# A hybrid decoder step: conditioning weights in rows of 256 columns, norm parameters on another queue, two tiles' split weights in another pool

## The chip, the core and the metric

The kernel runs on one core of a Trainium2 chip. Its time is the device time of one execution in microseconds (us), smaller is better. The engines are named as the profile names them: PE is TensorE's matrix multiply and PEld its weight load, DVE is VectorE, ACT is ScalarE, POOL is GpSimd, SP is SyncE. A "q" behind a name (SPq) is the engine's sequencer or DMA queue. Each engine carries out its own instructions in order; engines wait for each other through semaphores. SP and GpSimd issue the DMA transfers of this kernel.

## What is computed

One step of a decoder layer with 1024 features (D) for 512 prompt tokens and 8 sample tokens, 520 columns in all. Cut to what matters here:

```python
cs = silu(c)                                  # 9 conditioning vectors: 1 prompt, 8 samples
mod = cs @ w_mod + b_mod                      # (9, 6*1024)
sh1, sc1, g1, sh2, sc2, g2 = split(mod, 6)
h = rmsnorm(x, norm1_g) * (1 + sc1) + sh1
u = h @ w_in                                  # 8 parts of 1024 columns
...                                           # HGRN2 and RG-LRU on the parts of u
x = x + g1 * (merged @ w_out)
h2 = rmsnorm(x, norm2_g) * (1 + sc2) + sh2
x = x + g2 * (square(relu(h2 @ w_ff1)) @ w_ff2)
y = rmsnorm(x, final_norm_g)
```

The first norm needs sc1 and sh1, parts 1 and 0 of `mod`: 2048 columns of `w_mod`, 8 MiB of float32.

## The kernel before, in words

Activations lie transposed: features over the 128 partitions in 8 column tiles (`KO` = 8), tokens along the free axis. A product with fp32 accuracy is made of three: weight and activation are each split into a high part (rounded to the fast fp32r type) and a low part (the rest), and TensorE adds high x high, high x low and low x high (`products`, L115). A weight tile of 1024 x 128 comes in by one transfer from SP (`_load_w`, L66, buffer `wst`, 4 of them), ScalarE casts the high part (L75) and VectorE subtracts for the low part (L78), which makes `whi` and `wlo`. `split_place` says where these go: pool `whl` has two places, 0 and 2, taken in turn; later, when pool `sw` is open, four places are taken in turn. A tile of weights is 48 TensorE instructions, in two halves of 260 columns.

The head of the program is `begin`. It loads c (L325, L326) and x (L391, L393), then the conditioning weights: `load_mod(k)` (L1432) fills one of 8 buffers `wm` (`NWM`) of 1024 x 256, with 128 columns of part 1 and 128 of part 0 for column tile k, by two transfers. In between stand the loads of the first two weight tiles of `w_in` (columns f and q of the first head). `parameters_mod` (L276) loads `b_mod`, `norm1_g` and `norm2_g` by three small transfers from SP into a tile `ra`; `bounds` (L232, L233) loads two other small tensors from GpSimd into a tile of the same name, which has one buffer in the pool, and `parameters` (L293 to L300) loads the rest, also from GpSimd. `parameters_mod_in` transposes the first of these (L222) into `pm`.

`mod` makes one group of conditioning products (L356): 16 matmuls for two column tiles. ScalarE evacuates them (L358), TensorE transposes (L372), VectorE reduces (L376) and adds bias and gain (L380) into `modT`. The first group is followed by `scale_x` (L415, L417), which multiplies x by its row scales; `transposed(k)` (L426, L427) turns a column tile of x round. Four groups (`LEAD`) are written ahead of `transposed_s` (L434), which turns the sample rows; the other four stand in the loop over column tiles. There `affine_split(k)` makes the operand tile h[k] (ACT L447; DVE L448, L449; the 8 sample columns on POOL L443 to L445), and `products` of the first two weight tiles follow for column tile k, into two accumulators `mm` in PSUM.

Then `begin` closes pool `start`, which holds x, `wm` and the small tiles, and opens `hg` over the same memory; the first writers of `hg` are two memsets on GpSimd (L1481, L1484), the load of the first head's state (L458) and the sigmoids of the first head (L137), which also empty the first accumulator, so that the third weight tile can use it. From there eight heads follow, each with the state update on VectorE and ScalarE beside TensorE's products, then branches, output projection and the MLP, whose weights come in under a plan of their own (`schedule`), which starts from the places that the last splits took.

The order of the instructions on each engine is made by the build, from priorities and a simulated timeline; `behind` and `issue_after` pin single ones.

Of the kernel before, what the change touches and what calls it, by code (L numbers as in the profile page):

```python
# [6 lines left out]
F32 = mybir.dt.float32  # L7
F32R = mybir.dt.float32r
# [3 lines left out]
OP = mybir.AluOpType  # L12
# [8 lines left out]
KO = D // 128  # L21
# [8 lines left out]
NWM = 8  # L30
# [18 lines left out]
class Kernel:  # L49
# [31 lines left out]
    def split_place(self):  # L81
# [1 line left out]
        self.nsplit += 1  # L83
        self.places.append(self.nsplit % 4 if self.sw else 2 * (self.nsplit % 2))
        return self.places[-1]

    def load_split(self, key, stage):
        return self._split_w(self._load_w(key, stage), self.split_place())

    def take_w(self, key):  # L90
        n = self.wcur
# [179 lines left out]

    def parameters_mod(self):

        r = self.start.tile([64, 128], F32, name="ra")
        for a, b, name in ((0, 48, "b_mod"), (48, 56, "norm1_g"), (56, 64, "norm2_g")):
            self.nc.sync.dma_start(r[a:b], self.rows8(self.i[name]))  # L276
        return r

    def parameters_mod_in(self, r):
# [1140 lines left out]
    def begin(self):  # L1420

        nc = self.nc
        self.start = self.open_pool("start", 1)
        self.load_c()
        self.identity()
        mk = [((1, k), (0, k)) for k in range(KO)]
        raw = {}

        def load_mod(k):
            raw[k] = self.start.tile([128, KO, 256], F32, name="wm", bufs=NWM)  # L1430
            for j, (w, r, c, _) in enumerate(self.mod_key(*p) for p in mk[k]):
                nc.sync.dma_start(raw[k][:, :, j * 128:(j + 1) * 128],  # L1432
                                  w[r:r + 1024, c:c + 128].rearrange("(k p) n -> p k n", p=128))

        self.load_x()
        self.cond()
        self.bounds()
        pm = self.parameters_mod()
        load_mod(0)
        first = [self.load_split(self.head_cols(0)[0], self.wst)]  # L1440
        load_mod(1)
        first.append(self.load_split(self.head_cols(0)[1], self.wst))
        for k in range(2, KO):
            load_mod(k)
        self.norm_x()
        self.constants()
        par = self.parameters()
        self.decays()
        self.parameters_mod_in(pm)
        evac = self.mod(mk[0], raw.pop(0))  # L1450
        with self.tc.issue_after(evac.ins):
            self.scale_x()
        x = [self.transposed(k) for k in range(3)]
        for k in range(1, LEAD):
            self.mod(mk[k], raw.pop(k))
        hi, lo = (self.act.tile([128, KO, T2], F32R, tag="h", name="h", bufs=2) for _ in range(2))
        self.h = [(hi[:, k, :T], lo[:, k, :T]) for k in range(KO)]
        pss = self.transposed_s()
        xs = self.start.tile([128, KO * NB], F32, name="xhs")
        nc.vector.tensor_copy(xs, pss[:, :KO * NB])  # L1460
        acc = [self.pmm.tile([128, 2, 512], F32, name="mm") for _ in range(2)]
        for k in range(KO):
            if k + LEAD < KO:
                evac = self.mod(mk[k + LEAD], raw.pop(k + LEAD))
            if k + 3 < KO:
                x.append(self.transposed(k + 3))
            self.split_last = self.affine_split(k, x[k], xs[:, k * NB:(k + 1) * NB])
            if k:
                for j in (0, 1) if k == 1 else (k,):
                    for ps, (wh, wl) in zip(acc, first):  # L1470
                        self.products(ps, (wh[:, j], wl[:, j]), self.h[j], j == 0, j == KO - 1)
                        self.behind(self.last_product, evac)
        self.parameters_in(*par)
        self.first = acc
        self.close_pool()
        self.hg = self.open_pool("hg", 2)
        self.ppt_free = False
        self.at = []
        self.fkq = [self.hg.tile([128, 3, 32], F32, name=f"fkq{n}", bufs=1) for n in range(2)]
        for t in self.fkq:  # L1480
            nc.gpsimd.memset(t, 0.0)  # L1481
        for n in range(2):
            a = self.hg.tile([128, NC, C], F32, name=f"at{n}", bufs=1)
            nc.gpsimd.memset(a, 0.0)  # L1484
            self.at.append(a)
# [54 lines left out]
```

## Time and profile before

| what | value |
|---|---|
| median of 3 runs | 1044.82 us (1044.5 to 1045.27) |
| the profiled execution, in all | 1044.54 us |
| its span, from first to last instruction | 1042.6 us |
| TensorE (PE) busy | 1005.1 us, 96% |
| VectorE / ScalarE / GpSimd busy | 694.9 / 526.1 / 112.8 us |
| bytes read from HBM | 123.61 MB |
| mean granted TensorE clock | 0.996 |

How to read what follows. In a timeline a line has start, duration, engine, line of the code, operation, output and inputs with their shapes, and the count of merged instructions; in brackets how long the engine sat idle before it and what ended that. In a group of instructions the columns are busy time, mean duration in ns, idle time before them and what ended most of it. The chain of waits is the work that ended last, followed back from the end. In a list of waits stand the total, the number and the longest. A DMA stretch gives packets, bytes and the mean rate; a queue's line gives packets, MB and the share of 16 engines' time (transfers overlap, so it can be over 100%).

### The profile page before, as it was taken

How to read it: one execution, taken by the hardware profiler on the slowest of the kernel's cores; microseconds unless marked ns; L12 is line 12 of the kernel's file. 1: busy time of each engine (PE TensorE's matmuls, PEld its weight loads, DVE VectorE, ACT ScalarE, POOL GpSimd, SP SyncE). 2: the span in 40 equal slices, each digit the busy share in tenths (PEclk: the TensorE clock that was granted, in tenths of full speed). 3: DMA queues.
4: the chain of work that ended last, by engine and by line, in shares of the span. 5: the costliest groups of instructions: out<-in, count | busy, mean ns of one | idle time of the engine just before them, and what ended most of it. 6: DMA issues, size and time to landing. Idle time of an engine off the chain costs nothing.

```text
span 1042.6 us, 24269 instructions
## 1 busy us (share of the span) xinstructions
PE 1005.1 (96%) x9940; PEld 968.5 (93%) x9940; DVE 694.9 (67%) x1583; ACT 526.1 (50%) x1020; POOL 112.8 (11%) x215
## 2 busy tenths in 40 slices
PE   2999999999999999999999999999999999999995
PEld 1799999999999999989999999999999999999994
DVE  7558688695867768465333337767767676777775
ACT  5445753573574456342122224366555655656653
POOL 2200000000000000020000000011422231232040
PEclk9999999999999999999999999999999999999998
DMA  9963344343434324496555578332572484274242
GB/s 277 260 178 107 110 134 115 112 136 114 126 116 126 113 82 135 137 312 178 163 157 157 157 217 234 93 97 67 124 181 70 100 174 125 52 158 96 62 81 83
DMA packets 247792, 143.71 MB, mean 138 GB/s; under 512 B 6622, under 2 KB 242326, under 8 KB 247674
## 3 DMA queue, kind: packets, MB, share of 16 engines
q1 hardware_dynamic: 237874, 130.28, 44.1%
q0 software_dynamic: 9808, 11.89, 6.3%
q8 instruction: 78, 1.28, 0.5%
q14 instruction: 32, 0.26, 0.1%
HBM read 123.61 MB, written 11.26 MB: 129 GB/s over the span
## 4 chain that ended last, share of the span: by engine, by line
PE 90%; DMA 3%; SPq 3%; ACT 1%; DVE 1%; issue 1%; DVEq 0%; ACTq 0%
PE mm L115 65%; PE ps L1085 8%; PE pt L1085 4%; PE pb L1085 2%; PE ps L356 2%; SPq L1432 2%; PE pb L702 1%; PE ps L561 1%; DMA wst<-in_w_branch_a_dram 1%; DMA wst<-in_w_in_dram 1%; DMA wm<-in_w_mod_dram 1%; PE mm L1085 1%; PE pt L645 1%; PE pt L634 1%; PE ps L529 1%
## 5 line engine op out<-in xcount | busy, mean ns | idle before, releaser
L115 PE MATMUL mm<-h,whi 128*128 128x260 f32 (+1 forms) x3072 | 513.9, 286 | 1.4 <-ACT X L137 1.4
L115 PEld LDWEIGHTS mm<-h,whi 128*128 128x128 f32 x3072 | 427.3, 188 | 7.0 <-issue 3.4
L115 PE MATMUL mm<-h,wlo 128*128 128x260 f32 (+1 forms) x1536 | 316.4, 285 | 0.0
L75 ACT CAST whi<-wst 128x1024 fp32r<-128x1024 f32 x168 | 175.8, 1048 | 228.9 <-PE mm L115 175.4
L78 DVE TENSOR_TENSOR wlo<-wst,whi 128x1024 fp32r<-128x1024 f32 x168 | 205.1, 1222 | 91.2 <-ACT whi L75 90.1
L115 PEld LDWEIGHTS mm<-h,wlo 128*128 128x128 f32 x1536 | 240.0, 189 | 1.5 <-issue 1.0
L115 PE MATMUL mm<-a,whi 128*128 128x260 f32 x512 | 84.6, 285 | 0.0
L115 PEld LDWEIGHTS mm<-a,whi 128*128 128x128 f32 x512 | 70.6, 188 | 1.4 <-issue 1.4
L115 PE MATMUL mm<-a,wlo 128*128 128x260 f32 x256 | 52.3, 284 | 0.0
L797 POOL DMA_DIRECT2D t<-oaT_d x8 | 4.3, 550 | 399.2 <-ACT ma L137 389.0
L1181 DVE TENSOR_TENSOR f<-f 128x260 f32<-128x260 f32 x64 | 27.3, 427 | 28.3 <-ACT f L1176 27.6
L1170 ACT ACTIVATE ft<-ft,fsh 128x512 f32<-128x512 f32 (+2 forms) x36 | 24.0, 676 | 36.0 <-DVE ft L1167 36.0
L115 PE MATMUL mm<-b,whi 128*128 128x260 f32 x256 | 41.8, 285 | 0.0
L1173 POOL TENSOR_TENSOR ft<-ft,fsh 128x8 f32<-128x8 f32 x28 | 17.6, 629 | 219.0 <-DVE ft L1167 219.0
L115 PEld LDWEIGHTS mm<-a,wlo 128*128 128x128 f32 x256 | 39.5, 188 | 0.2 <-issue 0.2
L115 PEld LDWEIGHTS mm<-b,whi 128*128 128x128 f32 x256 | 35.0, 188 | 1.6 <-issue 1.6
L1215 POOL DMA_DIRECT2D ma<-snap x28 | 27.2, 971 | 35.2 <-issue 30.9
L1197 POOL DMA_DIRECT2D ma<-snap x28 | 26.2, 935 | 43.6 <-DMA ma<-snap 28.1
L813 DVE TENSOR_TENSOR t<-mm,t 128x520 f32<-128x520 f32 x8 | 5.6, 700 | 36.7 <-PE ps L372 36.7
L1176 ACT ACTIVATE f<-ft 128x520 f32<-128x520 f32 (+1 forms) x36 | 20.8, 587 | 14.4 <-POOL ft L1174 12.3
L376 DVE TENSOR_REDUCE mods<-ps 128x9 f32<-128x36 f32 x32 | 6.1, 192 | 31.4 <-PE ps L372 31.3
L115 PE MATMUL mm<-b,wlo 128*128 128x260 f32 x128 | 25.9, 283 | 0.0
(488 smaller groups left out, 1876.4 us busy)
## 6 DMA issues: line engine op xcount, KB each, us to landing
wst<-in_w_in_dram SPq DMA_DIRECT2D x64, 512.0 KB
wst<-in_w_mod_dram SPq DMA_DIRECT2D x32, 512.0 KB
wst<-in_w_ff_dram SPq DMA_DIRECT2D x64, 256.0 KB
wst<-in_w_ff_dram SPq DMA_DIRECT2D x32, 512.0 KB
wm<-in_w_mod_dram SPq DMA_DIRECT2D x16, 512.0 KB
st<-in_state_hgrn_dram SPq DMA_DIRECT2D x8, 512.0 KB
vb<-vd SPq DMA_DIRECT2D x8, 512.0 KB
out_dram<-st SPq DMA_DIRECT2D x8, 512.0 KB
```

Source lines behind the costliest of these rows:

```text
L75: ins = self.nc.scalar.copy(hi, st)
L78: self.nc.vector.tensor_tensor(lo, st, hi.bitcast(F32), OP.subtract)
L115: self.last_product = self.nc.tensor.matmul(ps[:, s, :c.stop - c.start], x, y[:, c], start=first and n == 0, stop=last and n == 2)
L356: nc.tensor.matmul(ps[r:r + 32, :n], self.cT[:, k, :], w[:, k, :], start=k < 4, stop=k >= KO - 4)
L1085: ins = self.nc.tensor.matmul(ps, x[:, w], y[:, f], start=j in (1, 7, 2) and k == 0 and n == 0, stop=k == 3 and n == 2, skip_group_check=True)
L1170: nc.scalar.activation(t[:, :p], t[:, :p], AF.Relu, bias=sh[:, 0:1])
L1173: eng.tensor_tensor(t[:, p:], t[:, p:], sh[:, 1:9], OP.add)
L1176: nc.scalar.activation(f, self.two(self.ft)[:, a:a + n], AF.Square)
L1181: self.nc.vector.tensor_tensor(f[:, n], f[:, a], f[:, b], op)
L1197: nc.gpsimd.dma_start(x[1][:, b], v[:, :n], accum_op=OP.add)
L1215: nc.gpsimd.dma_start(x[t][:, a], s[p], accum_op=OP.add)
L1432: nc.sync.dma_start(raw[k][:, :, j * 128:(j + 1) * 128], w[r:r + 1024, c:c + 128].rearrange("(k p) n -> p k n", p=128))
```

## The change

`mk`, the list of pairs that make a conditioning group, is regrouped: a group holds two neighbouring column tiles of one part, part 1 and part 0 in turn, where it held one column tile of both parts. So a `wm` buffer is 256 neighbouring columns and is loaded by one transfer. `parameters_mod` is called first, issues on GpSimd's queue and has a tile name of its own. The first two weight tiles are split into tiles of pool `start` by `first_w`, and no longer take a place through `split_place`. Their loads stand behind the second and third conditioning load instead of the first and second.

```diff
-    def load_split(self, key, stage):
-        return self._split_w(self._load_w(key, stage), self.split_place())
-
...
-        r = self.start.tile([64, 128], F32, name="ra")
+        r = self.start.tile([64, 128], F32, name="rm")
         for a, b, name in ((0, 48, "b_mod"), (48, 56, "norm1_g"), (56, 64, "norm2_g")):
-            self.nc.sync.dma_start(r[a:b], self.rows8(self.i[name]))
+            self.nc.gpsimd.dma_start(r[a:b], self.rows8(self.i[name]))
...
-        mk = [((1, k), (0, k)) for k in range(KO)]
+
+        mk = [((part, k), (part, k + 1)) for k in range(0, KO, 2) for part in (1, 0)]
         raw = {}
 
-        def load_mod(k):
-            raw[k] = self.start.tile([128, KO, 256], F32, name="wm", bufs=NWM)
-            for j, (w, r, c, _) in enumerate(self.mod_key(*p) for p in mk[k]):
-                nc.sync.dma_start(raw[k][:, :, j * 128:(j + 1) * 128],
-                                  w[r:r + 1024, c:c + 128].rearrange("(k p) n -> p k n", p=128))
-
+        def load_mod(n):
+            raw[n] = self.start.tile([128, KO, 256], F32, name="wm", bufs=NWM)
+            w, r, c, _ = self.mod_key(*mk[n][0])
+            nc.sync.dma_start(raw[n], w[r:r + 1024, c:c + 256].rearrange("(k p) n -> p k n", p=128))
+
+        def first_w(j):
+            st = self._load_w(self.head_cols(0)[j], self.wst)
+            hi, lo = (self.start.tile([128, KO, 128], F32R, name=n, bufs=2) for n in ("whi", "wlo"))
+            nc.scalar.copy(hi, st)
+            nc.vector.tensor_tensor(lo, st, hi.bitcast(F32), OP.subtract)
+            return hi, lo
+
+        pm = self.parameters_mod()
         self.load_x()
         self.cond()
         self.bounds()
-        pm = self.parameters_mod()
         load_mod(0)
-        first = [self.load_split(self.head_cols(0)[0], self.wst)]
         load_mod(1)
-        first.append(self.load_split(self.head_cols(0)[1], self.wst))
-        for k in range(2, KO):
-            load_mod(k)
+        first = [first_w(0)]
+        load_mod(2)
+        first.append(first_w(1))
+        for n in range(3, KO):
+            load_mod(n)
```

## The prediction

> **What bounds the kernel now.** I read the page first, then the table of stretches, the chain of waits, and the timeline of the first 55 us.
>
> ```profile
> span 1042.6 us, 24269 instructions
> ...
> PE 1005.1 (96%) x9940; PEld 968.5 (93%) x9940; DVE 694.9 (67%) x1583; ACT 526.1 (50%) x1020; POOL 112.8 (11%) x215
> ```
>
> TensorE is busy for 96% of the span. The table of stretches (length; busy time and instructions of PE, PEld, DVE, ACT, POOL; clock; DMA share; GB/s) shows where the other 37 us lie.
>
> ```profile
> 0.00:17.00 17.00, 1.30 (x10) 1.18 (x10) 10.46 (x65) 8.98 (x16) 6.50 (x17) 1.00 0.93 270
> 17.00:53.00 36.00, 30.81 (x285) 22.03 (x285) 21.67 (x62) 17.50 (x29) 7.97 (x28) 1.00 1.08 264
> ...
> 55.00:300.00 245.00, 244.09 (x2827) 235.32 (x2826) 182.10 (x505) 132.30 (x293) 0.00 (x0) 1.00 0.43 123
> ...
> 680.00:1000.00 320.00, 319.69 (x2632) 319.47 (x2631) 229.15 (x364) 189.46 (x340) 80.72 (x135) 1.00 0.46 110
> ```
>
> The body idles 0.9 us in 245 and 0.3 in 320, so a microsecond saved ahead of it should reach the end, and none can be saved in it. The head is another matter: 15.7 us idle before 17 us, 5.2 more up to 53, with the DMA engines full. The chain of waits agrees: it runs through the issue queue of the conditioning weights (L1432) and one of their transfers.
>
> ```profile
> 27.38 1.74 SPq L1432
> 29.16 7.62 DMA wm<-in_w_mod_dram
> ...
> 38.57 2.88 PE mm L115 x24
> ...
> 54.27 15.62 PE mm L115 x128
> ```
>
> TensorE's timeline in the head, with idle time in brackets:
>
> ```profile
> 16.95 0.34 PE L222 MATMUL ps<-ident,ra 64*128 64x64 f32 x1 [9.91 <-DMA ra<-in_norm_g_dram]
> ...
> 25.85 1.07 PE L356 MATMUL ps<-wm,cT 128*32 128x256 f32 x16 [1.20 <-DMA wm<-in_w_mod_dram]
> ...
> 29.45 1.07 PE L356 MATMUL ps<-wm,cT 128*32 128x256 f32 x16 [0.32 <-DMA wm<-in_w_mod_dram]
> 30.45 0.66 PE L434 MATMUL ps<-ident,xsn 8*128 8x8 f32 x8
> ...
> 36.91 1.07 PE L356 MATMUL ps<-wm,cT 128*32 128x256 f32 x16 [1.07 <-DMA wm<-in_w_mod_dram]
> ...
> 44.23 1.07 PE L356 MATMUL ps<-wm,cT 128*32 128x256 f32 x16
> ...
> 52.47 0.41 PE L115 MATMUL mm<-h,wlo 128*128 128x260 f32 x2
> 54.27 0.75 PE L115 MATMUL mm<-h,whi 128*128 128x260 f32 x4 [1.40 <-ACT X L137]
> ```
>
> The third, fourth and sixth group of conditioning products start on a transfer's landing: 3.60 us apart for one pair of 524 kB tiles, 7.46 for two. At that pace the eighth lands at about 44.2, where its products start. Only after the fourth group can the sample rows be transposed (30.45), which the first complete operand tile needs; from there TensorE is nearly full to 52.88. So the head's end is the landing of the fourth pair plus TensorE's backlog behind it, with one wait on the sixth pair inside.
>
> **The change part by part.**
>
> *Rows of 256 columns.* The bytes stay at 8 x 1.049 MB; 16 transfers become 8, and a row grows from 512 to 1024 bytes. No transfer of the trace has rows of 1024 bytes. The nearest are the 512-byte stretch (12 to 40 us) and the one in which the prompt's rows of 4096 bytes load (4 to 9 us):
>
> ```profile
> DMA packets 16156, 8.15 MB, mean 291 GB/s; under 512 B 277, under 2 KB 16154, under 8 KB 16154
> ...
> q1 hardware_dynamic: 16152, 8.13, 120.2%
> ```
>
> ```profile
> DMA packets 775, 1.95 MB, mean 391 GB/s; under 512 B 191, under 2 KB 316, under 8 KB 775
> ...
> q1 hardware_dynamic: 597, 1.92, 97.4%
> ```
>
> One of 16 engines takes 16 x 28 us / 16152 = 27.7 ns for a packet of 503 bytes, and 16 x 5 us / 597 = 134 ns for one of 3216. A line through both is 8 ns a packet and 0.039 ns a byte; 1024 bytes then take 48 ns, or 340 GB/s. The bounds are 291 (the row length does nothing) and 391. I take 340, since the fixed part is what is halved. A pair then takes 3.08 us for 3.60: 0.52 us saved each (0 to 0.92). The fourth pair lands 4 x 0.52 = 2.1 us sooner (0 to 3.7), with as many bytes ahead of it as before, both weight tiles included. The sixth lands 3.1 sooner, 1.0 more than the backlog has moved, which leaves almost nothing of its 1.07 us wait: 1.0 more (0 to 1.1).
>
> [...]
>
> *Regrouping.* A pair of products now holds the scales of two column tiles, the next one their shifts. Same instructions; operand tile 4 now needs the sixth group where it needed the fifth. That costs nothing as long as the products of tiles 0 to 3 cover it: 48 at 2.88 us per 24, so 5.8 us, against the 3.7 us between the fifth group at about 33.2 (36.91 less one pair) and the sixth. Without the cover it would cost the 3.7.
>
> *Norm parameters on GpSimd's queue.* The 9.91 us wait at 16.95 is on three small transfers that stand on SP's queue behind a weight tile:
>
> ```profile
> 9.82 2.36 SPq L276 DMA_DIRECT2D ra<-in_b_mod_dram  x1
> ```
> ```profile
> 1.38 0.77 POOL L232 DMA_DIRECT2D ra<-in_hg_lower_dram  x1 [0.32 <-issue]
> ```
> ```profile
> DMA to landing us min/median/max: 3.1/3.8/4.5
> ```
> ```profile
> 8.00 0.19 ACT L245 ACTIVATE ptmp<-ptmp 128x8 f32<-128x8 f32 x1
> ```
>
> The second line is from the answer for the tile that these loads write: issue to landing. Ahead of GpSimd's other loads they land by about 1.4 + 3 x 0.77 + 4.5 = 8.2 us at the latest, and the first group waits only for its own pair, at 27.3 less three pairs and two weight tiles of 1.8 us: 14.5. TensorE can then do the prompt's transposes earlier, of which 16 still come after the fourth group:
>
> ```profile
> L426 PE MATMUL pb<-ident,xn 128*128 128x128 f32 x16 | 2.6, 283 | 0.5 <-ACT xn L427 0.5
> ```
>
> Whatever leaves the backlog is saved, 0 to 2.6 us; TensorE runs in the order that the build gave it, and scaling x still stands behind the first group, so I take 0.5. The three issues push the rest of GpSimd's queue back by three times at most 0.77 = 2.3 us: the two loads of L232/L233 first, behind which ScalarE's exponentials of 8.00 us stand ahead of two squares. The row scales then come up to 2.3 us later, still by about 17 us; cost 0, as a transfer at 29 decides. The parameters behind them are read after 45 us. SP loses three issues, but its queue is paced by full DMA engines, so nothing is gained there.
>
> *Split weights in the start pool.* Casts and subtractions of the first two tiles are the same ones, to another address; the first tile now loads behind the second pair, 3.1 us later, long before the products of 31 us. Tiles three and four no longer wait for the first two's buffers. The timelines of ScalarE, VectorE, GpSimd and SP at the seam:
>
> ```profile
> 52.17 1.05 ACT L75 CAST whi<-wst 128x1024 fp32r<-128x1024 f32 x1 [1.59 <-PE mm L115]
> 53.13 0.60 ACT L137 ACTIVATE e<-mm 128x520 f32<-128x520 f32 x1
> 53.62 0.60 ACT L137 ACTIVATE X<-mm 128x520 f32<-128x520 f32 x1
> ```
> ```profile
> 53.25 1.23 DVE L78 TENSOR_TENSOR wlo<-wst,whi 128x1024 fp32r<-128x1024 f32 x1 [1.57 <-ACT whi L75]
> ```
> ```profile
> 51.54 0.30 POOL L1481 MEMSET fkq<- 128x96 f32 x2 [0.90 <-DVE h L449]
> ```
> ```profile
> 51.50 0.37 SPq L458 DMA_DIRECT2D st<-in_state_hgrn_dram  x1
> ```
>
> The cast leaves the 1.40 us gap. But the next pool's first writers (memset, state load) start right after the last reader of the start pool; that reader is now the last product (52.88), no longer VectorE's last subtraction. The sigmoid that frees the accumulator writes a tile of that pool too, so it starts behind 52.88, and its pair takes 53.62 + 0.60 - 53.13 = 1.1 us plus a hop: I take 0.1 us gained (0 to 0.8, if it need not wait). The state load goes out 1.4 us later; behind it on SP stand the gate matrices and the seventh weight tile. Tiles three to six are loaded by then and give 4 x 48 products, 23 us of cover; if it were gone, the 1.4 us would show. The two early casts and subtractions (1.05 and 1.23 each) go into idle time, below with its releasers for 40 to 52 us:
>
> ```profile
> L447 ACT ACTIVATE h<-xn,modT 128x512 fp32r<-128x512 f32 x3 | 2.5, 818 | 6.5 <-DVE modT L380 6.5
> ```
> ```profile
> L376 DVE TENSOR_REDUCE mods<-pt 128x18 f32<-128x72 f32 x3 | 0.7, 233 | 5.3 <-PE pt L372 5.3
> ```
>
> Cost 0 there, up to 1.5 if they stand in front of the norm's own work. Later splits count from two less: the order of buffers shifts only where the third and fourth pair of buffers open, in a stretch without idle time; 0.
>
> *Sum.* 2.1 + 1.0 + 0.5 + 0.1 = 3.7 us less. The profiled execution took 1044.54 in all (1.94 outside its span), so 1040.8 for it; the median of the runs lies 0.28 above that execution, hence **1041.1**. By the bounds: 3.7 + 1.1 + 2.6 + 0.8 = 8.2 less, or 1.5 more: 1036.6 to 1046.3.
>
> **The rivals.**
>
> *The row length does nothing.* 291 GB/s stays, the fourth pair lands at 29.4, and 0.5 + 0.1 remain: 1044.2. For it: the DMA engines are full at 291 with packets all of one size, and the faster stretch also reads from another tensor. Against it: 27.7 and 134 ns leave room for a fixed part only.
>
> *Casts ahead of the norm.* ScalarE works in order, and in the trace it has already stood behind a cast whose tile had not landed:
>
> ```profile
> 16.02 1.04 ACT L75 CAST whi<-wst 128x1024 fp32r<-128x1024 f32 x1 [3.41 <-DMA wst<-in_w_in_dram]
> ```
>
> If both new casts stand ahead of the last evacuation, it waits for two tiles behind the eighth pair: 3.6 us of transfer and 1.05 of cast, then an estimated 2.9 for evacuation, transposes, reduction, affine step and split (two of them in the rows above; idle time between them not counted), and 2.88 for the last two tiles' products: 10.4 after a landing at 44.2 - 4.2 = 40.0. The end at 50.4 instead of 52.88 leaves 2.5 gained: 1042.3. Against it: the code traces the norm first.
>
> *A worse order in the heads (slower).* The build orders instructions by a simulated timeline, and the change moves its first 50 us. The list of waits shows one place where TensorE, in order, stands before a transpose (L534) for VectorE's last product of a head:
>
> ```profile
> PE pt L534 <- DVE e L663: 1.8, 3, 1.0
> ```
>
> It occurs in each of eight heads and costs in three. At the longest 1.0 in all eight it is 6.2 us more, and 2.5 more net: 1047.3. It outweighs the gain from four further heads on. For it: it is order alone that spares the other five. Against it: within the heads nothing is changed.
>
> **How the numbers follow.** Forecast 0.55 (with its own range 1038.8 to 1042.8: rates of 310 to 391), no gain from rows 0.22, casts ahead 0.10, worse order 0.13. A measurement of this kernel can tell about 0.2%, 2.1 us. Faster by more: 0.54 of the forecast and 0.06 of the casts, 0.60. Within: 0.22, 0.04 and some 0.02 of the rest, 0.28. Slower by more: 0.12. The range, 1037.0 to 1046.4, takes in the bounds and the first two rivals, and leaves out most of the last.
>
> **What would show it.** Eight transfers of 1 MB on L1432, with a rate near 340 GB/s where 291 stood; the parameters' transpose before 10 us and the first group near 14.5; the fourth group near 27.3; the last product of the first two tiles near 49.3; a gap of about 1.3 us behind it, with the sigmoids right after the last product. It is wrong if the rate stays at 291, if a cast stands on ScalarE behind a transfer between the last two evacuations, or if the stretch from the third tile to the end is over 1 us longer than now.

## The result, and the profile after

| | median, us | lowest to highest | executions |
|---|---|---|---|
| before | 1044.61 | 1043.88 to 1046.73 | 14 |
| changed | 1045.07 | 1042.11 to 1047.51 | 14 |

The ratio of changed to before is 1.0003, with an interval of 0.9993 to 1.0014: no difference that can be told. The predicted range holds the time; the predicted gain of 3.7 us isn't there. The changed kernel's executions spread over 5.4 us, those of before over 2.9. Its profiled execution took 1044.72 us in all, against 1044.54. Lines of the code up to `begin` count three less than before: L356 is now L353, L426 L423, L115 L112, L447 L444.

The page of the changed kernel, span and busy time:

```profile
span 1042.9 us, 24260 instructions
...
PE 1006.9 (97%) x9940; PEld 970.3 (93%) x9940; DVE 693.8 (67%) x1583; ACT 527.0 (51%) x1022; POOL 114.2 (11%) x218
```

The table of stretches, columns as before the change:

```profile
17.00:53.00 36.00, 31.75 (x283) 23.43 (x283) 24.46 (x93) 21.46 (x34) 7.06 (x24) 0.95 0.97 281
...
55.00:300.00 245.00, 244.32 (x2828) 235.61 (x2828) 180.62 (x504) 131.34 (x291) 0.00 (x0) 1.00 0.41 121
```

The body is as full as it was. In the head TensorE is busy for 0.9 us more and its granted clock is 0.95 where it was 1.00. The DMA engines between 12 and 40 us:

```profile
DMA packets 11003, 9.37 MB, mean 335 GB/s; under 512 B 219, under 2 KB 10945, under 8 KB 10993
```

That is 335 GB/s for 291, with weight tiles of 512-byte rows in the same stretch; where only the 1024-byte rows move, 26 to 28 us, it is 348. So the transfers did what was forecast. TensorE's timeline:

```profile
14.35 0.47 PE L423 MATMUL pb<-ident,xn 128*128 128x128 f32 x1 [10.28 <-DVE xn L414]
...
14.97 0.36 PE L219 MATMUL ps<-ident,rm 64*128 64x64 f32 x1
17.40 3.64 PE L353 MATMUL ps<-wm,cT 128*32 128x256 f32 x32 [2.07 <-DVE pl L220]
...
26.95 1.07 PE L353 MATMUL ps<-wm,cT 128*32 128x256 f32 x16 [0.87 <-DMA wm<-in_w_mod_dram]
...
39.81 1.07 PE L353 MATMUL ps<-wm,cT 128*32 128x256 f32 x16
...
47.01 0.43 PE L219 MATMUL ps<-ident,rd 96*128 96x96 f32 x2 [0.24 <-DVE pa L220]
...
48.99 0.51 PE L112 MATMUL mm<-h,whi 128*128 128x260 f32 x2 [0.72 <-DVE h L446]
...
50.43 1.50 PE L112 MATMUL mm<-h,whi 128*128 128x260 f32 x6
...
54.37 0.75 PE L112 MATMUL mm<-h,whi 128*128 128x260 f32 x4 [1.19 <-ACT X L134]
```

The fourth group starts at 26.95 (29.45 before) and the eighth at 39.81 (44.23), yet the third weight tile's first product starts at 54.37, where it started at 54.27. The gain was there at 27 us and had gone by 54. Where it went is read by laying the table of stretches from the end of the fourth group to the third tile side by side, first before, then changed:

```profile
30.45:54.27 23.82, 20.89 (x200) 17.06 (x196) 14.13 (x36) 10.08 (x19) 7.97 (x28) 1.00 1.00 247
```
```profile
27.95:54.37 26.42, 23.79 (x213) 19.95 (x209) 15.87 (x41) 13.84 (x24) 8.19 (x28) 0.94 0.86 244
```

The stretch is 2.60 us longer. TensorE is not idle in it for longer (2.63 for 2.93); it is busy for 2.90 more. Two things account for that. The groups of instructions in this stretch show 24 transposes of x behind the fourth group where 16 stood:

```profile
L423 PE MATMUL pb<-ident,xn 128*128 128x128 f32 x24 | 3.8, 275 | 0.0
```

The group's busy time was 2.6 us before, so eight more are 1.2 us. Two transposes of `mod` and two products of the first tiles have moved behind the fourth group with them. Neighbouring instructions overlap (24 at a mean of 275 ns are 6.6 us, against 3.8 of busy time), so the busy times of groups don't simply add up, and the 1.2 us stand as an estimate for all of these. Stretches of 2 us show the granted clock:

```profile
46.00:48.00 2.00, 1.67 (x13) 1.24 (x11) 1.86 (x8) 1.33 (x2) 0.88 (x4) 1.00 0.78 207
48.00:50.00 2.00, 1.28 (x9) 1.08 (x8) 1.55 (x4) 0.58 (x2) 0.00 (x0) 0.89 0.61 180
50.00:52.00 2.00, 2.00 (x11) 2.00 (x11) 0.00 (x0) 0.90 (x1) 0.00 (x0) 0.50 0.01 4
52.00:54.00 2.00, 1.18 (x6) 0.93 (x5) 0.14 (x1) 0.78 (x2) 0.76 (x4) 0.75 0.00 0
```

0.89 and 0.75 as means of 1 and 0.5 put the half clock at 49.56 to 53.0, 3.4 us, in which TensorE was busy throughout: half of that, 1.7 us, is lost, an estimate from the clock. The six products at 50.43 take 1.50 us; six such products took 0.97 before. (The column prints 1.00 also ahead of the first change of clock that was recorded. There the lengths of equal products tell more: in the kernel before, the first conditioning group at 17.21 takes 1.93 us and the third at 25.85 takes 1.07. By the lengths of the groups between, an estimate, TensorE came to its full clock at about 20.9 us before and at 22.3 in the change.) 1.2 + 1.7 = 2.9, the further busy time. So 2.5 us from the landing and 0.3 of idle time were gained, 2.9 were lost, and the head of the traced execution ends 0.1 us later.

ScalarE, GpSimd and SP of the changed kernel at the seam:

```profile
41.04 1.05 ACT L75 CAST whi<-wst 128x1024 fp32r<-128x1024 f32 x1 [0.54 <-DMA wst<-in_w_in_dram]
42.00 0.36 ACT L355 COPY modev<-ps 128x256 f32<-128x256 f32 x1
...
46.66 1.52 ACT L444 ACTIVATE h<-xn,modT 128x512 fp32r<-128x512 f32 x2 [2.31 <-DVE modT L377]
49.61 1.28 ACT L134 ACT_TABLE_LOAD   x1 [1.42 <-DMA wst<-in_w_in_dram]
53.22 0.60 ACT L134 ACTIVATE e<-mm 128x520 f32<-128x520 f32 x1 [2.32 <-PE mm L112]
```
```profile
53.24 0.30 POOL L1486 MEMSET fkq<- 128x96 f32 x2 [5.66 <-PE mm L112]
```
```profile
53.21 0.37 SPq L455 DMA_DIRECT2D st<-in_state_hgrn_dram  x1
```

The first sigmoid, the next pool's memset and the state's load all start right behind the last product (53.18), as forecast. A cast stands ahead of the last group's evacuation (42.00), and one step, L444 at 46.66, makes two operand tiles out of that group. The table load at 49.61 wasn't forecast. Its cause stands on ScalarE earlier:

```profile
18.40 1.04 ACT L1435 CAST whi<-wst 128x1024 fp32r<-128x1024 f32 x1 [5.80 <-DMA wst<-in_w_in_dram]
19.46 1.28 ACT L242 ACT_TABLE_LOAD   x1
20.76 0.21 ACT L242 ACTIVATE ptmp<-ptmp 128x8 f32<-128x8 f32 x1
```

The exponentials, at 8.00 before, now stand behind the table load on the line of a sigmoid (L402, 1.28 us at 11.10). A further load of 1.28 us stands right ahead of them, at 19.46, and one more ahead of the first head's sigmoids, at 49.61. The kernel before has the load of L402 (there L405, at 11.12) and neither of these two; with the exponentials back at 8.2 us, in an experiment below, both are gone.

### The profile page after: what moved, and what is told of

Its sections match the earlier page's. It is cut to its first block, busy times and chain, and to the rows that moved or that the text cites. A ratio compares the mean times of both kernels' runs of the same rounds, so it can differ in the third digit from the quotient of the medians.

```text
span 1042.9 us, 24260 instructions
## 1 busy us (share of the span) xinstructions
PE 1006.9 (97%) x9940; PEld 970.3 (93%) x9940; DVE 693.8 (67%) x1583; ACT 527.0 (51%) x1022; POOL 114.2 (11%) x218
## 3 DMA queue, kind: packets, MB, share of 16 engines
q8 instruction: 78, 1.28, 0.5%
## 4 chain that ended last, share of the span: by engine, by line
PE 90%; DMA 3%; DVE 3%; SPq 2%; ACT 1%; issue 1%; DVEq 0%; ACTq 0%
PE mm L112 65%; PE ps L1082 8%; PE pt L1082 4%; PE ps L353 2%; PE pb L1082 2%; PE pb L699 1%; DMA wm<-in_w_mod_dram 1%; PE ps L558 1%; DMA wst<-in_w_in_dram 1%; SPq L1430 1%; PE mm L1082 1%; PE pt L642 1%; PE pt L631 1%; SPq L66 1%; DVE wlo L78 1%
## 5 line engine op out<-in xcount | busy, mean ns | idle before, releaser
L112 PE MATMUL mm<-h,whi 128*128 128x260 f32 (+1 forms) x3072 | 515.5, 286 | 2.0 <-ACT X L134 1.2
L112 PEld LDWEIGHTS mm<-h,whi 128*128 128x128 f32 x3072 | 428.5, 189 | 7.2 <-issue 3.4
L112 PE MATMUL mm<-h,wlo 128*128 128x260 f32 (+1 forms) x1536 | 317.2, 285 | 0.0
L75 ACT CAST whi<-wst 128x1024 fp32r<-128x1024 f32 x166 | 173.7, 1048 | 220.4 <-PE mm L112 175.8
L78 DVE TENSOR_TENSOR wlo<-wst,whi 128x1024 fp32r<-128x1024 f32 x166 | 202.6, 1221 | 91.7 <-ACT whi L75 90.0
L112 PEld LDWEIGHTS mm<-h,wlo 128*128 128x128 f32 x1536 | 240.7, 189 | 2.0 <-issue 1.4
L112 PE MATMUL mm<-a,whi 128*128 128x260 f32 x512 | 85.1, 286 | 0.0
L112 PEld LDWEIGHTS mm<-a,whi 128*128 128x128 f32 x512 | 70.7, 188 | 1.4 <-issue 1.4
L112 PE MATMUL mm<-a,wlo 128*128 128x260 f32 x256 | 52.0, 284 | 0.0
L1178 DVE TENSOR_TENSOR f<-f 128x260 f32<-128x260 f32 x64 | 27.3, 426 | 28.9 <-ACT f L1173 28.2
L112 PE MATMUL mm<-b,whi 128*128 128x260 f32 x256 | 41.8, 285 | 0.0
L112 PEld LDWEIGHTS mm<-a,wlo 128*128 128x128 f32 x256 | 39.4, 188 | 0.2 <-issue 0.2
L112 PEld LDWEIGHTS mm<-b,whi 128*128 128x128 f32 x256 | 35.0, 188 | 1.6 <-issue 1.6
L519 ACT ACTIVATE st<-st,fkq 128x128 f32<-128x128 f32 x64 | 20.0, 390 | 13.0 <-DVE fkq L498 10.5
```

Source lines behind the costliest of these rows:

```text
L75: ins = self.nc.scalar.copy(hi, st)
L78: self.nc.vector.tensor_tensor(lo, st, hi.bitcast(F32), OP.subtract)
L112: self.last_product = self.nc.tensor.matmul(ps[:, s, :c.stop - c.start], x, y[:, c], start=first and n == 0, stop=last and n == 2)
L519: nc.scalar.activation(st[:, b], st[:, b], AF.Copy, scale=fkq[:, 0, b:b + 1])
L1178: self.nc.vector.tensor_tensor(f[:, n], f[:, a], f[:, b], op)
```

## The experiments

The first theory: the rows and the placing are worth what was forecast up to 27 us, and the head loses it again between 28 and 54 us, because the last two column tiles share one group and TensorE runs thin there. The rival: one of the other edits (parameters, pool) costs what the rows gain. Each edit was first run alone on top of the kernel before (median 1044.79 on that chip), beside the whole change with its last groups undone.

**The rows alone.**

```diff
-        mk = [((1, k), (0, k)) for k in range(KO)]
+        mk = [((part, k), (part, k + 1)) for k in range(0, KO, 2) for part in (1, 0)]
...
+            nc.sync.dma_start(raw[n], w[r:r + 1024, c:c + 256].rearrange("(k p) n -> p k n", p=128))
```

> The rows and the regrouping alone; norm parameters on SP and split weights in their old pool. If the rows carry the gain and the last group, which two column tiles now need, gives it back (first theory): a rate near 348 GB/s while the pairs load, the eighth group near 40 us instead of 44.2, TensorE idle by about 1 us between the last group's transposes and the last tiles' products, and in some executions a stretch of half clock of 3.4 us there: times spread over 1042 to 1047 as with the whole change. If the other two parts lose what the rows gain (rival): 1040.5 to 1042, with a spread as small as before's.

Measured: median 1044.48, ratio 1.0001 (0.9991 to 1.0012). TensorE's timeline:

```profile
27.40 1.07 PE L356 MATMUL ps<-wm,cT 128*32 128x256 f32 x16
...
49.51 0.50 PE L115 MATMUL mm<-h,whi 128*128 128x260 f32 x2 [0.70 <-DVE h L449]
...
50.57 0.88 PE L115 MATMUL mm<-h,whi 128*128 128x260 f32 x6
...
53.58 0.75 PE L115 MATMUL mm<-h,whi 128*128 128x260 f32 x4 [1.42 <-ACT X L137]
```

The fourth group is 2.05 us earlier, the third tile only 0.69. The wait of 0.70 ahead of the last products is there without the other edits, and so are the 24 transposes behind the fourth group, but not the half clock: six products take 0.88. From the end of the fourth group (28.40) to the third tile TensorE is busy for 22.68 us, 1.8 more than before, all of it at full clock. So the regrouping by itself gives back two thirds of the gain in this execution; of the 0.69 the execution kept nothing (span 1043.2), since from the third tile to the end it took 989.6 where before took 988.3.

**The parameters alone on GpSimd's queue**, first there.

```diff
-            self.nc.sync.dma_start(r[a:b], self.rows8(self.i[name]))
+            self.nc.gpsimd.dma_start(r[a:b], self.rows8(self.i[name]))
...
+        pm = self.parameters_mod()
         self.load_x()
         self.cond()
         self.bounds()
-        pm = self.parameters_mod()
```

> The norm parameters on GpSimd's queue alone. First theory: the front of the head has slack, the fourth group still lands at 29.4 us, 1044.2 to 1045.0, spread as before. Rival: the parameters' transpose moves behind those of x in TensorE's order and costs 1 us or more: above 1045.5.

Measured: median 1047.96 of five executions, ratio 1.0031 (1.0019 to 1.0043), slower by 3.2 us. The rival had the loss but another cause: the parameters' transpose runs at 9.40 us, ahead of the first of x at 14.49. ScalarE, then TensorE:

```profile
17.41 1.28 ACT L245 ACT_TABLE_LOAD   x1
...
54.78 1.28 ACT L137 ACT_TABLE_LOAD   x1
```
```profile
20.09 1.94 PE L356 MATMUL ps<-wm,cT 128*32 128x256 f32 x16 [2.27 <-DVE ptmp L247]
...
57.22 0.75 PE L115 MATMUL mm<-h,whi 128*128 128x260 f32 x4 [2.83 <-ACT X L137]
```

Here the second table load falls between the last product and the sigmoid, and the gap is 2.83 us in place of 1.40. The third tile is 2.95 later; the other half of that arose in the head, where the first load stands ahead of the exponentials, the second group waits 2.27 for VectorE's steps behind them and takes 1.94 us for 1.27, by its length at half clock. In the whole change the second load fell at 49.61, where ScalarE was idle, and cost nothing that the trace shows: its cover is that the casts have left this place.

**The pool alone.**

```diff
+        def first_w(j):
+            st = self._load_w(self.head_cols(0)[j], self.wst)
+            hi, lo = (self.start.tile([128, KO, 128], F32R, name=n, bufs=2) for n in ("whi", "wlo"))
...
-        first = [self.load_split(self.head_cols(0)[0], self.wst)]
+        first = [first_w(0)]
```

> The split weights in the start pool alone. First theory: the gap ahead of the third tile goes from 1.40 to about 1.2 us and nothing else moves: 1044.2 to 1044.8. Rival: the early casts stand on ScalarE in front of the norm's work and the memset, state load and sigmoids wait for the last product: 1045.5 or more.

Measured: median 1046.19, ratio 1.0012 (1.0003 to 1.002), slower by 1.4 us. ScalarE, then TensorE:

```profile
45.46 1.05 ACT L75 CAST whi<-wst 128x1024 fp32r<-128x1024 f32 x1 [2.20 <-DMA wst<-in_w_in_dram]
46.41 0.36 ACT L358 COPY modev<-ps 128x256 f32<-128x256 f32 x1
```
```profile
55.57 0.74 PE L115 MATMUL mm<-h,whi 128*128 128x260 f32 x4 [1.19 <-ACT X L137]
```

This is the rival of the casts ahead of the norm, with one of the two casts ahead of the evacuation: ScalarE waits 2.20 us for a weight tile's landing with the last group's evacuation behind it. The gap at the seam shrinks by 0.2, the third tile starts 1.3 later.

**The whole change, with the last two groups in the old form**, so that each of the last two column tiles has a group of its own:

```diff
-        mk = [((part, k), (part, k + 1)) for k in range(0, KO, 2) for part in (1, 0)]
+        mk = [((part, k), (part, k + 1)) for k in range(0, KO - 2, 2) for part in (1, 0)]
+        mk += [((1, k), (0, k)) for k in (KO - 2, KO - 1)]
```

> The whole change, but groups seven and eight in the old form (one column tile each, rows of 512 bytes). First theory: those two pairs land about 1 us later, but tile 6 no longer waits for the eighth group; TensorE's idle time of about 1 us in front of the last products goes, and with it the stretch of half clock: 1041.5 to 1043.5, spread under 2 us. Rival (the pairing of the last tiles is not the cause): 1044 to 1047 with the spread of the whole change.

Measured: median 1043.76, ratio 0.9989 (0.998 to 0.9998).

```profile
40.42 1.07 PE L353 MATMUL ps<-wm,cT 128*32 128x256 f32 x16 [0.64 <-DMA wm<-in_w_mod_dram]
...
52.48 0.75 PE L112 MATMUL mm<-h,whi 128*128 128x260 f32 x4 [1.24 <-ACT X L134]
```

The eighth group is 0.6 later than in the change and the third tile 1.9 earlier: no wait stands ahead of the last products, and the granted clock is 1.00 all through this stretch. Most of the 1.9 is the clock. From the end of the fourth group (27.85) to the third tile it takes 24.63 us, 0.8 more than before, where the change takes 2.6 more. So the waits go with the shared last group, and in the change the half clock came with it; the rows alone have the group without the half clock. The median agrees, though it lies a little above the 1041.5 to 1043.5 that were expected, and its interval overlaps that of the change. With the runs of the single edits, the rival holds as well: both of its costs are real where the edits stand alone. The next four kernels, on another chip (before: median 1045.42), took those costs away one by one.

**The whole change, parameters behind the bounds' loads on GpSimd:**

```diff
-        pm = self.parameters_mod()
         self.load_x()
         self.cond()
         self.bounds()
+        pm = self.parameters_mod()
```

> The whole change, but the three norm parameters stand on GpSimd's queue behind the two loads of bounds instead of ahead of them. Theory: ahead of them they push bounds' exponentials behind the change of ScalarE's table to the sigmoid, so that two more table loads of 1.28 us stand on ScalarE and bounds' work on VectorE and TensorE stands in front of the first group; behind them the exponentials run before 9 us again and both loads go. The parameters alone cost 3.2 us against before, so 1042 to 1044 here, the third tile 1 to 2 us sooner than in an execution of the whole change at full clock. Rival (the slack of the front hides this in the whole change): 1045, the same as the whole change.

Measured: median 1047.11, ratio 1.0014 (1.0005 to 1.0023): a miss. The table loads are gone, the exponentials are back at 8.2 us, and the first group starts 2.2 us sooner. But:

```profile
15.18 1.93 PE L353 MATMUL ps<-wm,cT 128*32 128x256 f32 x16
...
22.79 1.93 PE L353 MATMUL ps<-wm,cT 128*32 128x256 f32 x16 [2.06 <-DMA wm<-in_w_mod_dram]
...
27.63 1.94 PE L353 MATMUL ps<-wm,cT 128*32 128x256 f32 x16
...
54.62 0.74 PE L112 MATMUL mm<-h,whi 128*128 128x260 f32 x4 [1.19 <-ACT X L134]
```

All four early groups take 1.93 us in place of 1.07, the half clock's length, up to 29.5 us. With the wait of 2.07 us gone, TensorE's early work stands spread out, with idle time between the groups, where the change has two groups back to back. The third tile is no earlier than in the change. The execution that was traced was the fastest of the eleven, 1044.60 us; why the median lies 2.5 above it, no trace shows.

**The whole change, split weights in their old places** (the loads behind the second and third conditioning load, as in the change):

```diff
-        first = [first_w(0)]
+        first = [self.load_split(self.head_cols(0)[0], self.wst)]
```

> The whole change without the pool of its own: the first two tiles' split weights take places 2 and 0 again. Theory: the early casts of tiles three and four leave the norm's stretch, which took 1.3 us of the pool's own experiment, but the third tile's cast (1.05 us) and the table load (1.28 us) now stand between the last product and the sigmoid: gap 2.5 to 2.9 us instead of 1.2, in sum 1044.5 to 1046.5. Rival (the early casts cost nothing here): 1046 to 1047.

Measured: median 1045.72, ratio 1.0006 (0.9997 to 1.0015). ScalarE, then TensorE:

```profile
50.02 1.05 ACT L75 CAST whi<-wst 128x1024 fp32r<-128x1024 f32 x1 [2.39 <-PE mm L115]
51.09 1.28 ACT L137 ACT_TABLE_LOAD   x1
```
```profile
46.98 0.88 PE L115 MATMUL mm<-h,whi 128*128 128x260 f32 x4 [0.29 <-ACT h L447]
...
53.53 1.23 PE L115 MATMUL mm<-h,whi 128*128 128x260 f32 x4 [2.84 <-ACT X L137]
```

Cast and table load stand together in the gap, 2.84 us, after which TensorE runs at half clock (four products in 1.23 us for 0.75, and a granted clock of 0.50 from 54 to 58 us). So the own pool takes the cast out of the gap in the whole change, and gives the table load its cover. It has a price there too: without it the last products wait for 0.29 us, where the change waits for 0.24 and 0.72, and they end at 50.70 at full clock, 2.5 us before those of the change. This kernel has the shared last group as well, so how long the last products wait hangs on the order around it too. In the medians, 1.0006 and 1.0003 of the kernel before, the pool is neither a gain nor a loss that can be told.

**All three**: rows for six groups and the old form for the last two, parameters behind the bounds' loads, old places.

> Rows of 256 columns for six groups, the last two groups in the old form, norm parameters on GpSimd behind bounds' loads, old places for the first two tiles. Theory (each of the three losses has its own cause): no second table load, no early casts, no idle time ahead of the last products: third tile near 51.5, 1041 to 1042.5. Rival (the losses overlap or a new order brings its own): 1043 or more.

Measured: median 1043.4, ratio 0.9983 (0.9972 to 0.9994), 1.8 us faster than before by the ratio, the lowest of all kernels here, but above the 1041 to 1042.5 that were expected.

```profile
27.01 1.94 PE L356 MATMUL ps<-wm,cT 128*32 128x256 f32 x16
...
52.40 0.75 PE L115 MATMUL mm<-h,whi 128*128 128x260 f32 x4 [1.42 <-ACT X L137]
```

The third tile is 1.87 us earlier than before (near 51.5 was expected), and about as much arrives in the median, although the fourth group still takes 1.94 us, by its length at half clock.

**The same with the own pool.**

> As the last one, but with the pool of its own for the first two tiles' split weights. Theory: casts of tiles three and four stand on ScalarE in the norm's stretch again and cost up to 1.3 us there, against 0.2 us won at the gap: 0.5 to 1.2 us slower than with the old places, 1041.8 to 1043.5. Rival: the pool is worth its 0.2 us and is equal or faster.

Measured: median 1045.74, ratio 0.9998 (0.9986 to 1.001), 2.3 us above its sister on the same chip, though the two intervals overlap; 0.5 to 1.2 were expected. In the traced execution a wait for the norm's operand is back in the last products, and the third tile starts at 53.56, 1.16 later:

```profile
50.35 1.30 PE L112 MATMUL mm<-h,whi 128*128 128x260 f32 x6 [0.53 <-ACT h L444]
```

With no table load to cover, the pool looks like a loss, though not one clear of noise.

**An earlier full clock.** From the miss came a third theory: what the head lacks is TensorE at full clock from the first group on, and some work for it beforehand would give that, which the author assumed and no run had shown. Four kernels got 11 further products of the identity with the conditioning vectors, 256 columns each, at about 7 to 14 us, into an accumulator that nobody reads (before: median 1044.82 on that chip).

```diff
+        warm = self.cT.rearrange("p k b -> p (k b)")
+        pw = self.ppt.tile([128, 512], F32, name="pt")
+        for _ in range(11):
+            nc.tensor.matmul(pw[:, :256], self.ident, warm, start=True, stop=True)
         load_mod(0)
```

The change with it, the best version with it, the kernel before with it, and the change with parameters behind the bounds' loads with it:

> The whole change plus 11 products of the identity with the transposed conditioning (no result is used), on TensorE between the transposes of c and the first transposes of x, where it idles for 10 us. [...] With the extra products the full clock comes before 16 us, the groups at 15 to 27 us take 1.07 us each instead of up to 1.94, and the slow half of the executions goes: median 1042.5 to 1044, against 1045.1. Rival (the spread comes from the idle stretch ahead of the last products alone): median and spread unchanged.

> Rows for six groups, old form for two, norm parameters behind bounds' loads, old places, plus the same 11 extra products. Theory: full clock before 16 us instead of 29.6; median 1040.5 to 1042, all executions within 1.5 us of it: faster than before by 0.25% or more. Rival (the clock of the front is hidden behind the transfers): 1043, as without them.

> The kernel before plus the same 11 extra products. Theory: there the work starts at 17 us and is dense, full clock comes at 20.9, and the fourth group waits for its transfer at 29.4 all the same: 1043.8 to 1044.8, no difference that can be told. Rival (the clock's start is worth something by itself): 1043 or less.

> The whole change with the norm parameters behind bounds' loads, plus the same 11 extra products. Theory: without them this had full clock only at 29.5 us and a ratio of 1.0014 to before; with them before 16 us, the fourth group takes 1.07 us on landing, and 2.5 us or more are gained: ratio 0.998 to 0.999. Rival (its loss came from the order, not from the clock): ratio 1.001 again.

Measured: 1046.91 (ratio 1.0021, 1.0007 to 1.0036), 1046.56 (1.0022, 1.0009 to 1.0034), 1046.51 (1.0016, 1.0008 to 1.0025) and 1047.89 (1.003, 1.0017 to 1.0043): all slower than the kernel before, and all four expectations missed. The theory fell. Stretches of the kernel before, without and with the further products:

```profile
22.00:26.00 4.00, 1.45 (x12) 0.80 (x14) 3.25 (x10) 3.30 (x6) 0.00 (x0) 1.00 1.20 290
```
```profile
18.00:22.00 4.00, 3.23 (x25) 1.32 (x21) 3.96 (x13) 2.46 (x3) 0.00 (x0) 0.61 1.20 287
22.00:26.00 4.00, 3.38 (x15) 2.16 (x12) 2.58 (x8) 3.59 (x6) 0.00 (x0) 0.50 1.20 291
```

The full clock does come early, by the length of the first conditioning group (1.07 us at 17.03, before 1.93 at 17.21). But the stretch from 14 to 18 us is thin, with TensorE busy for 1.84 of its 4.00 us, and the clock falls to half from 18.9 to 29.1, while the kernel before has it full from 20.9 on, by the estimate above. In the other three it falls in the same way, for 6.8 to 10.2 us. How much of the losses this is, the traces don't show. In the kernel before with the products, the third tile starts 0.36 us later, and 1.5 more are lost behind it at full clock. Of the last of the four only the fastest execution was traced, 1043.72 us, which loses nothing.

## Why the prediction was right and wrong

The range, 1037.0 to 1046.4, holds the time because it was wide enough for a full gain and for none at all; that is no credit to the forecast inside it, and the rival that came nearest in time, 1044.2, had a cause that didn't happen. The sum was 3.7 us less; the head of the traced execution ended 0.1 later. The 3.8 between are 1.7 from the clock, 1.7 from the transposes of x and what moved with them (1.2 lost for 0.5 gained) and 0.8 from idle time (0.3 gained for 1.0 + 0.1), less 0.4 by which the landing was better (2.5 for 2.1).

**Rows of 256 columns: right.** 340 GB/s were taken, 348 measured; the fourth group was forecast near 27.3 and came at 26.95, the eighth's pair near 40.0 and its products at 39.81. Rows of twice the size moved 348 GB/s for 291. The 310 at the foot of the forecast's own range was the author's estimate; no run shows it.

**TensorE's clock: no term and no rival.** The rows quoted showed 1.00 in the head, even where the first group took 1.93 us, by its length at half clock (the third took 1.07), and the forecast took that as given, for a stretch that it made thinner itself. The 1.7 us lost are as large as any term of the sum but the first. The half clock lasted from 49.56 to 53.0; in the 3.41 us ahead of it TensorE was not without work, but busy for 2.36.

**"I take 0.5" (transposes of x): wrong sign.** More of them should have gone ahead of the fourth group; eight more went behind it. The rows alone show the same 24, so it comes with the new groups, in the order that the build made for them. The first group came at 17.40 and not at 14.5, and the parameters were transposed at 14.97 and not before 10. Their landing was forecast rightly (8.2 at the latest; GpSimd's last wait for them ends at 7.99). But scaling x, which was to stay behind the first group, went ahead of it: a transpose of x stands first on TensorE and waits for it until 14.35, and then TensorE waits 2.07 us more for VectorE's copies, which stand behind the scaling and the masks.

**"That costs nothing" (regrouping) and the 1.0 of the sixth pair: wrong.** The cover was counted for operand tile 4 and it held there. It wasn't counted for the last two tiles: they now hang on one group, so the two norm steps come together (46.66), and what was gained from the wait on the sixth pair came back as waits of 0.24 and 0.72 ahead of the last products. Undoing the last pair took these waits away, and the half clock with them.

**"Cost 0" (exponentials behind GpSimd's three issues): wrong reason.** They were counted as a delay of 2.3 us, not as a change of place relative to a table load. Two further loads of 1.28 us each followed; alone this edit costs 3.2 us, and in the change the emptied seam hides the second load.

**Split weights in the start pool: mechanism right, balance wrong.** The last product does gate the next pool's writers and the gap shrank by 0.2, where 0.1 was taken. But the rival that had 0.10, casts ahead of the norm, is what the pool does when it stands alone, at 1.4 us; beside the best version the median is 2.3 higher. A sign that the prediction gave against itself is there in the change as well: the cast at 41.04 waits 0.54 us for a transfer, with the last group's evacuation behind it. This cast alone delays nothing there, since TensorE takes up that group's transposes only at 45.65, without a wait. What the pool wins by covering the table load it loses again ahead of the seam, as the trace with the old places shows.

**The rivals.** The first and the last didn't happen: the waits of L534 didn't grow. The third tile to the end of the span took 988.5 us, before 988.3. In the other kernels it was 987.4 to 991.8, though. The three above 990 have a stretch of half clock behind the third tile (the change with split weights in their old places 0.50 from 54 to 58 us, the best version with further products 0.61 there, the change with further products 0.50 from 262 to 264); why a change to the head moves the body of the others by a microsecond either way was not tried out.

What is not settled: the executions of the changed kernel spread with their mean granted clock, 1042.11 to 1043.26 us at 0.996 for its three fastest, 1046.67 to 1047.51 at 0.993 for its four slowest. A half-clock stretch of 3.4 us takes 0.0016 off the mean and costs up to 1.7 us, so 0.003 would be two more such stretches. That is an estimate, since only one execution was traced, and a weak one: the mean also takes in the end of the kernel, where the clock is at 0.5 for the last 7 to 8 us and TensorE is busy for 0.00 of the last 9, and the clock doesn't order all executions. One at 0.994 took 1043.80, and those of the best version with the own pool took 1044.24 to 1046.43 at 0.997.

## What to carry to other kernels

A faster transfer ahead of an engine that works in order is worth only what the work behind it can follow (here the fourth group came 2.5 us sooner and the third tile 0.1 later): count that work again with the new grouping, the last group above all, and not with the old one. Moving three small transfers to another queue can move an activation across a table load (here two further loads of 1.28 us, and 3.2 us where it was done alone); look at what stands in order on both sides before calling it free. Several edits in one change should each be run alone: here the rows gained in the head and not in the time, two others lost, and one of these covered part of what the other cost.

## What the runs showed of the hardware

Where the profile of a head has it, the granted clock was 1.00 or 0.50: 0.50 for 3.4 us in the change, 6.8 with split weights in their old places and 6.8 to 10.2 in the early part where products were added. In stretches of 3.4 us laid from the changes of clock themselves, the one ahead of the fall in the change and the one behind the rise to full clock in the kernel before, which the lengths of the groups put at about 20.9 us, are:

```profile
46.16:49.57 3.41, 2.36 (x15) 1.73 (x15) 3.31 (x11) 1.52 (x2) 0.88 (x4) 1.00 0.76 211
```
```profile
20.92:24.34 3.42, 2.07 (x24) 1.10 (x17) 2.74 (x10) 2.92 (x5) 0.00 (x0) 1.00 1.21 290
```

TensorE was busy for 2.36 us and the clock fell to 0.50; it was busy for 2.07 and the clock stayed at 1.00. So its busy time in such a stretch does not decide by itself; what does, the runs don't show. The four kernels with work put in only to raise the clock were slower than the kernel before by 0.16 to 0.30%.

Transfers moved 291 GB/s with rows of 512 bytes, 348 with 1024 and 391 in a stretch with mostly 4096, which reads from another tensor.
